# A decoder trunk on one Trainium2 core: four output chunks of w_out under way, and unread products in TensorE's longer planned gaps

## The chip, the core and the metric

The kernel runs as one program on one of the eight cores of a Trainium2 chip (trn2). The metric is the device time of one execution in microseconds. The engines are named as the profile names them: PE is TensorE (matrix products; PEld is its loading of weights), DVE is VectorE, ACT is ScalarE, POOL is GpSimd, SP is SyncE, whose queue issues the DMAs.

## The reference, cut to what matters

One inference step of a two-layer decoder for 256 prompt positions and 8 sample positions, that is 264 columns under the same weights. Layer 0 mixes tokens with a Mamba-2 SSD block, layer 1 with dilated attention; each layer then attends into 256 memory tokens and ends with a gated feed-forward block.

```python
for i in range(DEPTH):
    u = rms_norm(x, g[0])
    mix = ssd_mixer(u, ...) if i % 2 == 0 else dilated_mixer(u, ...)
    x = x + rms_norm(mix, g[1])
    kv = memory_kv(mem, ...)                   # rms_norm(mem) @ w_kv
    x = x + rms_norm(cross_attn(rms_norm(x, g[2]), kv, w_q, w_o), g[3])
    x = x + rms_norm(conv_ffn(rms_norm(x, g[4]), ...), g[5])
```

The change concerns the end of `ssd_mixer`, and the gaps of TensorE everywhere:

```python
gated = y * silu(z)                            # (264, 2048), four groups of 512
gated = gated * rsqrt(mean(gated * gated, per group) + EPS)
out = (gated * norm_w) @ w_out                 # 2048 -> 1024
```

## The kernel before, in words

Activations lie with channels on the partitions and the 264 positions in the free dimension, in chunks of 128 channels. Every weight block (128 x 1024 numbers, 512 KB) comes by DMA into `raw`; ACT casts it to `hi`, and DVE takes `lo = raw - hi`. Activations are split likewise (`uh`, `ul`; `gh`, `gl` for w_out). A product is three passes, hi by h, hi by l and lo by h, so one block of eight sub-blocks is 24 products of 128 x 264 into one accumulator in PSUM. `product` does that for each output chunk; `wsplit` loads and splits the weights.

PSUM has eight banks under four tags: `mm` 2, `s` 2, `t` 3, `f` 1. An output chunk holds a bank from its first product until it has been read out. A chunk normally goes under `mm`, so two are under way at once. The list `head` names other tags for the next chunks: its entry `('t', 'f')` means a bank of tag `t`, with weights from the buffers `rawf`, `hif` and `lof`, which the memory work shares.

w_out has eight output chunks with 16 sub-blocks each, four per group of gates. Group 3 is gated last: its sum of squares goes through PE (tile `s`), ACT and DVE make the reciprocal root (`r`, `r2`), DVE scales `xs`, and ACT and DVE split the result into `gh` and `gl`. The last quarter of every output chunk waits for that. `memkv(l)` works out the keys and values of the memory tokens: the sums of squares (`rawf` by `ones`), their root `memr`, the scaled and split memory (`ld`, `mh`, `ml`), and products into the one bank `f`. It is recorded "aside", so the planner may put it wherever PE has room. The first cross-attention reads its result back from DRAM (`o_memk`, `o_memv`).

The order of work isn't the order of the program. `program` records operations; `Plan.rank` and `Plan.latest` give each a priority from assumed costs, and `Plan.order` places them engine by engine, the most urgent ready one first. `Plan.run` does so several times and issues the order that its own costs call shortest. Buffers of one tag are handed out in the order in which they were recorded. The planner also assumes that PE is half as fast after little work: it adds up planned columns in slices of its time (`columns`, against the constants `WINDOW` and `COLUMNS`) and doubles the cost of a product accordingly. Each engine then works strictly in the issued order, and a waiting instruction holds up all behind it. Every operation is issued by one statement, line 626, so the profile's rows are told apart by tile names: `mm<-gh,hi` is a w_out product, `mm<-uhl,hi` one of the other projections.

Of the kernel before, what the change touches and what calls it, by code (L numbers as in the profile page):

```python
# [7 lines left out]
F32 = mybir.dt.float32  # L8
# [115 lines left out]
class Pool:  # L124
# [9 lines left out]
    def tile(self, shape, dt=F32, tag=None, bufs=1, name=None):  # L134
        b = Buf(self.plan, tuple(shape), dt, self, tag or name, bufs)
        b.name = name
        b.slots = self.last.setdefault(b.tag, Slots(bufs))
        return b.view

    def __enter__(self):  # L140
# [38 lines left out]
class Plan:  # L179
    def __init__(self, nc, tc):  # L180
        import concourse.bacc as bacc
        self.nc, self.tc = nc, tc
        self._nc2 = bacc.Bacc("TRN2", target_bir_lowering=False, num_devices=1)
        self.ops, self.stack, self.closed, self.loose, self.k = [], [], [], [None], 0
        self.follows, self.lengths, self.first = None, [], 0
        self.vector, self.scalar = Engine(self, "DVE", nc.vector), Engine(self, "ACT", nc.scalar)
        self.gpsimd, self.tensor = Engine(self, "POOL", nc.gpsimd), Engine(self, "PE", nc.tensor)
        self.sync, self.either = Engine(self, "SP", nc.sync), Either(self)
# [235 lines left out]
    def order(self, emit):  # L424
# [8 lines left out]
        columns = {}  # L433
# [46 lines left out]
        def open_pool(p):  # L480
# [13 lines left out]
                p.real = p.ctx.__enter__()  # L494
            real_stack.append(p)

        for o in self.ops:
            if o.n == 0:
                admit(o)
        left = len(self.ops)  # L500
        while left:
            best = None
            for e in engs:
                w, r = wait[e], ready[e]
                while w and w[0][0] <= free[e]:
                    _, _, o = heapq.heappop(w)
# [5 lines left out]
                if r:  # L512
                    s = free[e]
                elif w:
                    s = w[0][0]
# [6 lines left out]
            s, e = best  # L522
            w, r = wait[e], ready[e]
            free[e] = s
            while w and w[0][0] <= s:
                _, _, o = heapq.heappop(w)
                heapq.heappush(r, (o.prio, o.seq, o))
            o = None
            if e == "ACT":
# [15 lines left out]
                o = pick[2]  # L545
            elif e == "PE" and HOLD:

                k = int(s / WINDOW)
                rate = 2.4 if columns.get(k - 1, 0.0) >= COLUMNS else 1.2
                room = columns.get(k, 0.0) + (WINDOW * (k + 1) - s) * rate - COLUMNS  # L550
# [21 lines left out]
                o = pick[2]  # L572
            else:
                o = heapq.heappop(r)[2]
# [10 lines left out]
            late = max([max(min(b.slots.free)[0], b.pool.opens()) for b in o.bufs if b.real is None], default=0.0)  # L585
# [4 lines left out]
            for b in o.bufs:  # L590
                if b.real is None:
                    open_pool(b.pool)
                    place_ = min(b.slots.free)
# [11 lines left out]
            if e in ("DVE", "POOL") and o.port[e]:  # L605
                s = max(s, port)
                port = s + ns
            if e == "PE":
                if part not in (None, o.part):
                    ns += CHANGE  # L610
                part = o.part

                ns *= 1 if columns.get(int(s / WINDOW) - 1, 0.0) >= COLUMNS else 2
                k = int((s + ns) / WINDOW)
                columns[k] = columns.get(k, 0.0) + o.columns
            o.end, o.took = s + ns, ns
            free[e] = o.end
            if e == "SP":
                dma = max(dma, s + 1300.0) + o.nbytes / 320.0
                o.end = dma + 1000.0  # L620
                free[e] = max(free[e], dma - BACKLOG)
            if call is not None and emit:
                f, a, k = call
                a = [v.real() if isinstance(v, View) else v for v in a]
                k = {n: v.real() if isinstance(v, View) else v for n, v in k.items()}
# [26 lines left out]
WINDOW = 10240 / 3  # L652
COLUMNS = 3060.0
# [6 lines left out]
LATE_D = -1e6  # L660
# [9 lines left out]
CHANGE = 100.0  # L670
STRETCH = 2.5
HOLD = 12
PASSES = 4
SPARES = 2000.0, 3000.0, 5000.0
SWITCHES = 2000.0, 4000.0
# [24 lines left out]
def program(plan, A):  # L700
    V, S, G, PE, D, E = plan.vector, plan.scalar, plan.gpsimd, plan.tensor, plan.sync, plan.either
    with ExitStack() as ctx:
# [37 lines left out]
        x = ap_.tile([P, KD, T], F32, tag="x", name="x")  # L740
# [10 lines left out]
        D.dma_start(out=idf, in_=A["ident"])  # L751
        identr = cp.tile([P, P], F32R, name="identr")
        S.copy(identr, idf)
        ident = identr.bitcast(F32)

        idn2f = load(cp, "idn2")
# [23 lines left out]
        def product(w, kk, chunks, xh, xl, consume, late=None):  # L780

            for j in chunks:

                tag, own = head.pop(0) if head else ("mm", "")
                acc = pm.tile([P, 512], F32, tag=tag, name=nm("mm"), bufs=BANKS[tag])[:, :T]
                wv = w[j].rearrange("p (k c) -> p k c", k=kk)
                for k0 in range(0, kk, 8):
                    kn = min(8, kk - k0)
                    hi, lo = wsplit(wv[:, k0:k0 + kn, :], own, (2, 2) if own else (4, 3), late=late)
                    for k in range(kn):  # L790
                        PE.matmul(acc, hi[:, k, :], xh[:, k0 + k, :], start=k0 + k == 0, stop=False)
                        PE.matmul(acc, hi[:, k, :], xl[:, k0 + k, :], start=False, stop=False)
                        PE.matmul(acc, lo[:, k, :], xh[:, k0 + k, :], start=False, stop=k0 + k == kk - 1)
                consume(j, acc)
# [141 lines left out]
        def ssd(uh, ul, r):  # L936
            with plan.pool("ssd") as sp:
# [149 lines left out]
                t = small()  # L1087
# [157 lines left out]
                    pass  # L1245
                D.dma_start(out=A["o_pconv"], in_=pconv)
                D.dma_start(out=A["o_sconv"], in_=hist[:, :, 1:4, :])
                with plan.aside():
                    memkv(0)
                post = Post(1)  # L1250
                product(A["w_out"], 16, range(8), gh, gl, post, late=LATE_D)
                return post.finish(2)

        def states(pool):
# [663 lines left out]
```

## Time and profile before

| | |
|---|---|
| median of three runs | 1140.64 us (1138.1 to 1141.13) |
| the profiled execution | 1134.57 us |
| its span, first to last instruction | 1132.8 us |
| PE busy | 1032.3 us, 91% |
| DVE busy | 889.2 us, 78% |
| ACT busy | 642.2 us, 57% |
| mean granted clock of TensorE | 0.958 |

The profiled execution is 1.77 us longer than its span and 6.07 us shorter than the median of the other runs. In the rows below, busy time is what an engine worked in a stretch; the idle time in square brackets in a row of the timeline is what the engine waited just before it, with the instruction that ended the wait. PEclk is the granted clock as a share of full speed: 1.00 is 2.4 GHz and 0.50 is 1.2 GHz.

### The profile page before, as it was taken

What the parts mean: (1) busy time and instruction counts of PE and PEld (TensorE: products, weight loads), DVE (VectorE), ACT (ScalarE), POOL (GpSimd) and SP (SyncE); (2) the same over time, 40 slices, a digit from 0 to 9 for tenths busy, and PEclk for the clock granted to TensorE, in tenths of its full rate; (3) what the DMA queues carried; (4) which work ended last, traced back from release to release, by engine and by line L of the source; (5) the groups of instructions that cost most, each with busy time, mean ns of one, the idle gap of its engine ahead of it and who ended that gap; (6) DMA issues with size and microseconds to landing.
All of it is one profiled execution on the core that took longest, in us unless ns stands there. A gap on an engine that the chain in (4) does not pass through costs nothing.

```text
span 1132.8 us, 21191 instructions
## 1 busy us (share of the span) xinstructions
PE 1032.3 (91%) x7895; PEld 982.9 (87%) x7895; DVE 889.2 (78%) x2060; ACT 642.2 (57%) x1271; POOL 66.9 (6%) x142
## 2 busy tenths in 40 slices
PE   6799978979998698999999999999896989999995
PEld 6799866979988597999999999989795879999995
DVE  7989999974889889999954685574899778777544
ACT  7887665664644378777644554344544356555442
POOL 0221110000000000222200000000000001000000
PEclk9899988989999899999999999998998889999998
DMA  9234545665898876888767876676589336878761
GB/s 311 85 113 161 175 130 170 216 224 182 292 320 292 287 266 191 274 281 277 269 198 217 277 282 241 223 282 238 182 303 327 130 112 224 279 270 287 263 177 53
DMA packets 80599, 257.20 MB, mean 227 GB/s; under 512 B 16952, under 2 KB 21848, under 8 KB 79344
## 3 DMA queue, kind: packets, MB, share of 16 engines
q1 hardware_dynamic: 80496, 255.85, 66.6%
q8 instruction: 62, 1.02, 0.3%
q14 instruction: 41, 0.34, 0.1%
HBM read 238.70 MB, written 44.34 MB: 250 GB/s over the span
## 4 chain that ended last, share of the span: by engine, by line
PE 66%; DVE 18%; ACT 7%; DMA 6%; issue 3%; SPq 0%; DVEq 0%; ACTq 0%
PE mm L626 48%; PE s L626 7%; PE f L626 7%; DVE kv L626 4%; PE t L626 3%; DVE lo L626 3%; DMA o_sssm<-sto 2%; ACT hi L626 2%; DVE kvo L626 1%; DVE xs L626 1%; ACT L601 1%; ACT sto L626 1%; DVE yv L626 1%; DVE hif L626 1%; DMA raw<-w_in 1%
## 5 line engine op out<-in xcount | busy, mean ns | idle before, releaser
L626 PE MATMUL mm<-uhl,hi 128*128 128x264 f32 x2960 | 569.3, 290 | 33.5 <-ACT uhl L626 15.5
L626 PEld LDWEIGHTS mm<-uhl,hi 128*128 128x128 f32 x2960 | 468.6, 191 | 42.9 <-ACT uhl L626 17.3
L626 DVE TENSOR_TENSOR lo<-raw,hi 128x1024 fp32r<-128x1024 f32 (+1 forms) x283 | 338.4, 1197 | 136.5 <-ACT hi L626 131.4
L626 PE MATMUL mm<-uhl,lo 128*128 128x264 f32 x1480 | 423.1, 287 | 1.4 <-DVE lo L626 1.4
L626 ACT CAST hi<-raw 128x1024 fp32r<-128x1024 f32 (+1 forms) x283 | 291.6, 1033 | 226.7 <-PE mm L626 182.7
L626 PEld LDWEIGHTS mm<-uhl,lo 128*128 128x128 f32 x1480 | 281.3, 190 | 2.3 <-DVE lo L626 1.9
L626 PE MATMUL mm<-mh,lo 128*128 128x264 f32 x352 | 100.2, 285 | 0.0
L626 PE MATMUL mm<-mh,hi 128*128 128x264 f32 x352 | 100.0, 284 | 0.0
L626 PE MATMUL mm<-ml,hi 128*128 128x264 f32 x352 | 99.9, 284 | 0.0
L626 DVE SCALAR_TENSOR_TENSOR kv<-kv,t 128x256 f32<-128x256 f32 x256 | 88.9, 416 | 7.7 <-PE t L626 7.4
L626 PEld LDWEIGHTS mm<-mh,lo 128*128 128x128 f32 x352 | 66.4, 189 | 0.0
L626 PEld LDWEIGHTS mm<-ml,hi 128*128 128x128 f32 x352 | 66.2, 188 | 0.0
L626 PEld LDWEIGHTS mm<-mh,hi 128*128 128x128 f32 x352 | 66.2, 188 | 0.0
L626 PE MATMUL f<-mh,hi 128*128 128x256 f32 x128 | 39.0, 304 | 7.7 <-ACT hi L626 4.7
L626 ACT ACTIVATE sto<-t,sdt 128x128 f32<-128x128 f32 x128 | 37.9, 389 | 12.3 <-DMA o_sssm<-sto 11.0
L626 POOL COPY pst<-gr 128x2 f32<-128x2 f32 x44 | 27.0, 613 | 281.7 <-DVE gr L626 281.6
L626 PE MATMUL mm<-gh,hi 128*128 128x264 f32 x128 | 37.5, 296 | 6.3 <-ACT gh L626 6.3
L626 DVE SCALAR_TENSOR_TENSOR gy<-gr,ld,gy 128x255 f32<-128x255 f32 (+1 forms) x88 | 42.0, 480 | 1.0 <-ACT gy L626 0.8
L626 PE MATMUL f<-hi,ml 128*128 128x256 f32 x128 | 37.3, 291 | 3.2 <-ACT kvo L626 3.2
L626 PE MATMUL f<-hi,mh 128*128 128x256 f32 x128 | 37.3, 292 | 2.9 <-ACT kvo L626 2.9
L626 PE MATMUL f<-lo,mh 128*128 128x256 f32 x128 | 37.2, 290 | 2.7 <-DVE lo L626 1.6
L626 PE MATMUL f<-mh,lo 128*128 128x256 f32 x128 | 38.5, 301 | 0.5 <-DVE lo L626 0.5
(284 smaller groups left out, 1702.6 us busy)
## 6 DMA issues: line engine op xcount, KB each, us to landing
raw<-ffn_gu SPq DMA_DIRECT2D x88, 512.0 KB, 4.6
raw<-w_in SPq DMA_DIRECT2D x40, 512.0 KB, 3.7
kv<-cmk SPq DMA_DIRECT2D x32, 512.0 KB, 5.7
kv<-cmv SPq DMA_DIRECT2D x32, 512.0 KB, 5.9
raw<-ffn_d SPq DMA_DIRECT2D x32, 512.0 KB, 4.0
o_sc<-cache SPq DMA_DIRECT2D x16, 1022.0 KB, 8.3
raw<-w_qkv SPq DMA_DIRECT2D x18, 512.0 KB, 5.6
rawf<-state SPq DMA_DIRECT2D x16, 512.0 KB, 4.4
```

Of the source, the lines that this page charges most:

```text
L601: self.nc.scalar.preload_act_table_set(o.table)
L626: f(*a, **k)
```

## The change

Two things are changed. First, `ssd` records the product of w_out before the memory work of layer 0, and `head` gives its first four output chunks banks of their own: two under `mm`, two under `t`, the fourth with weights from the buffers of the memory work. Second, `order` calls a new function, `warm`, before it places an instruction on PE. Where PE's planned wait, shortened to 70 per cent, is at least 500 ns, and a bank of some tag is free at its start, it issues as many 512-column products of the identity matrix by itself as fit, at an assumed 215 or 430 ns each, and lets the planner count them. Nobody reads the result; the bank goes back afterwards. These tiles are named `keep`.

```diff
@@ class Pool, tile
         b.slots = self.last.setdefault(b.tag, Slots(bufs))
+        if self.psum:
+            self.plan.banks.setdefault(b.tag, b)
@@ class Plan, __init__
+        self.keep, self.banks, self.kept = None, {}, []
@@ class Plan, order
+        def warm(a, s):
+
+            s = a + FILL * (s - a)
+            tags = [(t, x.slots) for t, x in self.banks.items() if x.slots.free and min(x.slots.free)[0] <= a]
+            if s - a < GAP or not tags:
+                return a, ()
+            tag, slots = min(tags, key=lambda t: min(t[1].free)[0])
+            room, out = [], None
+            while True:
+                ns = (215.0 if columns.get(int(a / WINDOW) - 1, 0.0) >= COLUMNS else 430.0)
+                if a + ns > s:
+                    break
+                a += ns
+                room.append((int(a / WINDOW), 512.0))
+                if emit:
+                    if out is None:
+                        x = self.banks[tag]
+                        out = x.pool.real.tile([128, 512], F32, tag=tag, bufs=x.bufs, name="keep%d" % len(self.kept))
+                        self.kept.append(out)
+                    v = self.keep[0].real()
+                    self.nc.tensor.matmul(out, v, v.unsqueeze(1).to_broadcast([128, 4, 128]), start=True, stop=True)
+            if room:
+                place_ = min(slots.free)
+                slots.free.remove(place_)
+                slots.free.append((a + 380.0, place_[1], None))
+            return a, room
+
         for o in self.ops:
             if o.n == 0:
                 admit(o)
...
             if e == "PE":
+                if self.keep is not None and self.keep[1].end is not None:
+                    t, room = warm(max(last, self.keep[1].end + 300.0), s)
+                    if room:
+                        for k, n in room:
+                            columns[k] = columns.get(k, 0.0) + n
...
+FILL = 0.7
+GAP = 500.0
@@ program
         S.copy(identr, idf)
+        plan.keep = identr, plan.ops[-1]
@@ ssd
+                post = Post(1)
+                head[:] = [('mm', ''), ('mm', ''), ('t', ''), ('t', 'f')]
+                product(A["w_out"], 16, range(8), gh, gl, post, late=LATE_D)
                 with plan.aside():
                     memkv(0)
-                post = Post(1)
-                product(A["w_out"], 16, range(8), gh, gl, post, late=LATE_D)
```

The new order has 222 of these products in 46 groups, the longest of 17, 15, 14, 14, 14 and 10. Since the planner plans anew around them, other instructions move too. Three places follow. The first is PE at the end of gating. The tiles `mm_...<-gh` are output chunks of w_out; `s_451` is the sum of squares of group 3, `gh_454` is the scaled group 3 that comes of it, and `f_459<-rawf` are the sums of squares of the memory. Before:

```order
L626 MATMUL mm_558_2761<-gh_445_2780,lo_564_2789 128x264
L626 MATMUL f_459_2765<-rawf_465_2774,ones_60 128x256
L626 MATMUL s_451_2859<-sq_447_2803,ones_60 128x264
L626 MATMUL s_451_2859<-sq_450_2835,ones_60 128x264
L626 MATMUL f_459_2765<-rawf_467_2827,ones_60 128x256 x2
L626 MATMUL mm_550_2720<-gh_454_2889,hi_555_2678 128x264
```

And now, with two chunks more, `mm_473` and `mm_481`, the first three rows and the last five of the same stretch:

```order
L664 MATMUL s_451_2937<-sq_447_2895,ones_60 128x264
L664 MATMUL s_451_2937<-sq_450_2921,ones_60 128x264
L664 MATMUL mm_465_2849<-gh_445_2874,lo_471_2917 128x264
...
L664 MATMUL mm_481_2926<-gh_398_2528,lo_484_2941 128x264
L664 MATMUL mm_481_2926<-gh_398_2528,hi_483_2766 128x264
L664 MATMUL mm_481_2926<-gl_399_2533,hi_483_2766 128x264
L664 MATMUL mm_457_2805<-gh_454_3014,hi_462_2749 128x264
L664 MATMUL mm_465_2849<-gh_454_3014,hi_470_2852 128x264
```

Between the sum of group 3 and the first product that needs group 3 there were two rows of memory sums, and now there are 52 products of w_out; the memory sums stand some 200 products later. The second place is DVE at the same point: `r2` and `r` are the reciprocal root of group 3, `xs` the scaling by it, `memr` and `ld` belong to the memory, and `lo` is a weight split. Before:

```order
L626 TENSOR_TENSOR sq_447_2803<-sq_447_2803,sq_449_2816 128x264
L626 SCALAR_TENSOR_TENSOR r2_453_2875<-s_451_2859,r_452_2865 128x264
L626 SCALAR_TENSOR_TENSOR kvo_468_2877<-f_459_2765,memr_2871 128x256
L626 SCALAR_TENSOR_TENSOR r2_453_2875<-r2_453_2875,r_452_2865 128x264
L626 SCALAR_TENSOR_TENSOR kvo_468_2877<-kvo_468_2877,memr_2871 128x256
L626 SCALAR_TENSOR_TENSOR r_452_2865<-r2_453_2875,r_452_2865 128x264
L626 SCALAR_TENSOR_TENSOR memr_2871<-kvo_468_2877,memr_2871 128x256
L626 TENSOR_TENSOR xs_28_2087<-xs_28_2087,r_452_2865 128x1056
L626 SCALAR_TENSOR_TENSOR ld_469_2783<-ld_469_2783,ld_456_331,memr_2871 128x256 x2
L626 SCALAR_TENSOR_TENSOR ld_470_2838<-ld_470_2838,ld_456_331,memr_2871 128x256 x2
L626 SCALAR_TENSOR_TENSOR gl_455_2899<-xs_28_2087,ld_22_304,gh_454_2889 128x264 x4
```

Now:

```order
L664 TENSOR_TENSOR sq_447_2895<-sq_447_2895,sq_449_2906 128x264
L664 TENSOR_TENSOR lo_476_2934<-raw_474_2812,hi_475_2911 128x1024
L664 TENSOR_TENSOR lo_484_2941<-raw_482_2708,hi_483_2766 128x1024
L664 TENSOR_TENSOR lo_487_2957<-raw_485_2784,hi_486_2857 128x1024
L664 SCALAR_TENSOR_TENSOR r2_453_2980<-s_451_2937,r_452_2946 128x264
L664 SCALAR_TENSOR_TENSOR r2_453_2980<-r2_453_2980,r_452_2946 128x264
L664 SCALAR_TENSOR_TENSOR r_452_2946<-r2_453_2980,r_452_2946 128x264
L664 TENSOR_TENSOR xs_28_2132<-xs_28_2132,r_452_2946 128x1056
L664 TENSOR_TENSOR lo_479_3010<-raw_477_2841,hi_478_2991 128x1024
L664 SCALAR_TENSOR_TENSOR gl_455_3026<-xs_28_2132,ld_22_304,gh_454_3014 128x264 x4
```

The memory's seven operations have gone from between the sum and `gl`, and four weight splits for the new chunks have come, three of them ahead of the root. The third place is PE at the start of the last feed-forward block, where `s_1751` is the sum of squares after the cross-attention and the `mm` rows are the first products of the feed-forward block. Before:

```order
L626 MATMUL mm_1746_10935<-uhl_1692_10289,lo_1749_10880 128x264
L626 MATMUL s_1751_10970<-sq_1715_10745,ones_60 128x264
L626 MATMUL s_1751_10970<-sq_1750_10974,ones_60 128x264
L626 MATMUL mm_1770_10999<-uhl_1754_10993,hi_1772_10902 128x264
L626 MATMUL mm_1776_11002<-uhl_1754_10993,hi_1778_10937 128x264
```

Now:

```order
L664 MATMUL mm_1746_11181<-uhl_1692_10514,lo_1749_11126 128x264
L664 MATMUL s_1751_11216<-sq_1715_10987,ones_60 128x264
L520 MATMUL keep42_11225<-identr_136 128x512 x3
L664 MATMUL s_1751_11216<-sq_1750_11220,ones_60 128x264
L520 MATMUL keep43_11250<-identr_136 128x512 x14
L664 MATMUL mm_1770_11249<-uhl_1754_11243,hi_1772_11148 128x264
L664 MATMUL mm_1776_11267<-uhl_1754_11243,hi_1778_11183 128x264
```

Three and fourteen unread products have come into the chain, ahead of instructions that it waits for; the other rows stand as they did.

## Rows read from the trace of the kernel before

**Rows 1.** The page: busy time by engine, and the chain that ended last.
```profile
PE 1032.3 (91%) x7895; PEld 982.9 (87%) x7895; DVE 889.2 (78%) x2060; ACT 642.2 (57%) x1271; POOL 66.9 (6%) x142
PE 66%; DVE 18%; ACT 7%; DMA 6%; issue 3%; SPq 0%; DVEq 0%; ACTq 0%
```

**Rows 2.** Busy time by stage; columns: stretch, length, engines, PEclk, DMA share, GB/s.
```profile
60.00:120.00 60.00, 59.78 (x492) 56.82 (x492) 57.25 (x115) 46.63 (x93) 13.12 (x22) 1.00 0.47 156
120.00:213.00 93.00, 80.14 (x591) 70.09 (x591) 91.41 (x179) 52.03 (x100) 5.24 (x8) 0.91 0.50 157
213.00:228.00 15.00, 15.00 (x112) 14.56 (x112) 14.65 (x26) 13.96 (x21) 0.00 (x0) 1.00 0.69 231
284.00:360.00 76.00, 71.11 (x558) 68.57 (x558) 66.58 (x216) 40.03 (x80) 0.00 (x0) 1.00 0.89 306
924.00:960.00 36.00, 35.68 (x271) 35.29 (x272) 29.95 (x67) 22.00 (x42) 1.69 (x10) 0.94 0.45 160
```

**Rows 3.** Timeline of PE around the wait in w_out: start, us, instruction, [idle before].
```profile
228.15 1.05 PE L626 MATMUL s<-sq,ones 128*128 128x264 f32 x4
229.04 1.03 PE L626 MATMUL f<-rawf,ones 128*128 128x256 f32 x4
236.34 0.81 PE L626 MATMUL mm<-gh,hi 128*128 128x264 f32 x2 [6.28 <-ACT gh L626]
```

**Rows 4.** The chain that ended last, at full clock: start, us, what.
```profile
213.91 6.15 PE mm L626 x50
```

**Rows 5.** Timeline of DVE in the same wait, and one weight split from the chain.
```profile
230.92 0.43 DVE L626 SCALAR_TENSOR_TENSOR r<-s,r 128x264 f32<-128x264 f32 x1 [3.23 <-ACT r L626]
234.12 1.66 DVE L626 SCALAR_TENSOR_TENSOR ld<-ld,ld,memr 128x256 f32<-128x256 f32 x4
204.37 1.14 DVE lo L626
```

**Rows 6.** Stretches at half clock (columns as in rows 2); the sum is over all twelve.
```profile
37.67:44.50 6.83, 5.66 (x26) 5.69 (x27) 6.83 (x20) 5.89 (x14) 1.85 (x4) 0.50 0.00 1
160.55:170.79 10.24, 7.86 (x29) 6.21 (x30) 10.24 (x21) 3.25 (x8) 0.83 (x2) 0.50 0.63 133
191.27:198.10 6.83, 3.66 (x10) 1.99 (x11) 6.83 (x14) 3.06 (x7) 0.00 (x0) 0.50 0.03 11
232.23:242.47 10.24, 6.12 (x27) 6.10 (x28) 9.70 (x19) 7.22 (x14) 0.00 (x0) 0.50 0.35 122
382.42:392.66 10.24, 6.01 (x22) 5.27 (x23) 8.88 (x41) 2.00 (x5) 0.00 (x0) 0.50 0.92 354
430.21:433.62 3.41, 3.15 (x15) 2.84 (x14) 3.41 (x11) 3.06 (x9) 0.00 (x0) 0.50 0.89 292
873.94:887.59 13.65, 8.81 (x26) 6.72 (x27) 10.19 (x49) 4.89 (x15) 0.00 (x0) 0.50 0.75 264
921.73:928.55 6.82, 4.53 (x19) 4.49 (x20) 6.75 (x20) 3.25 (x9) 0.00 (x0) 0.50 0.17 64
sum 95.00, PE 62.86 PEld 55.00 DVE 75.14 ACT 36.59 POOL 2.68; mean PE 5.24 PEld 4.58 DVE 6.26 ACT 3.05 POOL 0.22
```

**Rows 7.** Timeline of PE: idle times, and 512-column products at full clock.
```profile
322.24 1.99 PE L626 MATMUL s<-ld,qT 128*128 128x256 f32 x8 [2.21 <-DMA ld<-o_memk]
422.91 1.05 PE L626 MATMUL t<-bB,sel 128*128 128x512 f32 x3
423.80 0.28 PE L626 MATMUL f<-mh,hi 128*128 128x256 f32 x1
429.25 0.50 PE L626 MATMUL t<-bB,sel 128*128 128x512 f32 x1 [3.41 <-ACT sto L626]
877.51 1.30 PE L626 MATMUL s<-identr,pp 128*128 128x128 f32 x4 [5.92 <-ACT pp L626]
924.02 1.47 PE L626 MATMUL mm<-uhl,hi 128*128 128x264 f32 x5 [4.13 <-ACT uhl L626]
```

**Rows 8.** The chain that ended last, in the cross-attention of layer 1.
```profile
882.74 7.73 PE s L626 x24
```

More of the change, by code (lines that the diff above doesn't have):

```diff
@@ L500, in order @@
         left = len(self.ops)
+        last = 0.0
         while left:
@@ L617, in order @@
             free[e] = o.end
+            if e == "PE":
+                last = o.end
             if e == "SP":
```

## The prediction

> **What bounds the kernel now.** I read the page first, then the busy time of the engines by stage, then the timeline of PE for its waits, and last the chain that ended last. On the page PE is busy for 1032.3 us of the span, 91%, and has two thirds of the chain [rows 1]. That average hides stages with other limits [rows 2]. From 120 to 213 us DVE works 91.41 us of 93 and PE 80.14: there DVE decides, and a quicker PE buys nothing. From 213 to 228 us, and from 924 to 960, PE is all but full and everything it doesn't have to do is worth its time. So a change to PE's waits and clock has to be priced stage by stage.
>
> The timeline of PE has few long waits. The longest are 6.28 us in w_out [rows 3], and 5.92 us and 4.13 us in and after the cross-attention of layer 1 [rows 7]. After such waits the granted clock falls: the half-clock stretches hold 95.00 us, in which PE is busy for 62.86 us [rows 6]. The last of them lies behind PE's last product and costs nothing.
>
> **w_out with four chunks.** In the trace PE sums the squares of group 3 at 228.15, finishes some memory sums, and then waits 6.28 us for `gh` [rows 3]. It had nothing left, because only two chunks were open and both had done their first three quarters. In the new order 52 products of two further chunks stand between that sum and the first product that needs group 3. Fifty such products took 6.15 us at full clock [rows 4], so 52 take 6.40 us, which fills the wait: 6.28 us go. With the wait goes the half clock behind it: from 232.23 to 242.47 PE is busy for 6.12 us [rows 6], which at 2.4 GHz in place of 1.2 would be 3.06 us. Together 9.3 us at the most.
>
> What comes late next is `gh` itself. Three weight splits now stand ahead of the root on DVE and one ahead of `gl`: 4 x 1.14 = 4.6 us [rows 5]. Seven memory operations have left: four took 1.66 us, and the three at 0.43 us like `r` are at most 1.3 us [rows 5]. That leaves DVE with some 1.6 us more, in a place where it sat idle for 3.23 us [rows 5]. If DVE is no earlier there than before, `gh` comes up to 1.6 us later than it did. On PE the memory's eight sums no longer lie ahead of that wait; of two passes each, at 1.03 us for four passes [rows 3], they are 4.1 us, which PE has done less of by then. So an idle rest of between 0 and 6.28 + 4.1 + 1.6 - 6.4 = 5.6 us can stay. I take 1.4 us, nearer to nothing: six of the eight stood ahead of group 3's sum, which is so issued 3.1 us earlier, and DVE's idle 3.23 us is more than its added work. Net gain 7.9 us, between 3.7 and 9.3. It is kept by what follows: w_out's end opens the next stage, and the loads of that stage wait for the buffers that w_out frees, so they move with it.
>
> **The unread products.** There are 222. I laid the groups beside the trace by the names of their neighbours: 22 groups with 136 products stand where PE waits, 24 groups with 86 where the trace shows no wait. Their length: three 512-column products start at 422.91 and the next product at 423.80, so 0.30 us each at the most [rows 7]. In a wait they cost nothing as long as they fit: 14 take at most 4.2 us, against 4.13 and 5.92.
>
> What they give is clock. A wait of 2.21 us stands in a stretch with PEclk 1.00 [rows 2, 7]; after 3.41 us the clock is at half from 430.21 [rows 6, 7]. Where the fill leaves less than that, I take the clock as kept.
>
> - After 924.02: the 14 fill the 4.13 us to the end, so 4.53 us of work at half clock [rows 6] becomes half as long: 2.3 us gained, on PE's path, since the products wait for nothing else there.
> - From 873.94 to 887.59: fourteen at 0.22 to 0.30 us leave 1.7 to 2.8 us of the 5.92, between the wait that kept the clock and the one that lost it. PE is busy 8.81 us in it and the chain runs over its 24 products of 7.73 us [rows 6, 8]. All of it would be 4.4 us; I take half, 2.2.
> - From 382.42 to 392.66: DVE is busy 8.88 of 10.24 us and PE 6.01 [rows 6]. At most 3.0 us; I take 0.9, since DVE sets the pace.
> - From 160.55 to 170.79 and from 191.27 to 198.10 DVE is busy to the last hundredth [rows 6]; from 37.67 to 44.50 also. Nothing, though the first product after the wait there could give up to 2.8 us.
>
> The 86 products outside a wait are work. Seventeen stand between 44 and 86 us and ten between 148 and 220. PE is full from 60 to 120, but its lateness falls to DVE, which is full after that and decides [rows 2]: nothing, with 17 x 0.30 = 5.1 us as the other end. Six of the ten stand at 214 to 221, where PE is full: 1.8 us in whole. Eleven stand at the start of the feed-forward block of layer 0 and in the memory work behind it, next to the wait of 3.41 us, and I take half, 1.6 us of 3.3. Seven stand at 941 to 945, where PE is busy 35.68 of 36 us [rows 2]: half again, 1.1 us of 2.1. The rest, in the two cross-attentions, wait beside DVE: nothing. Sum 4.5 us, between 0 and 12.3.
>
> **The sum.** -7.9 - 2.3 - 2.2 - 0.9 + 4.5 = -8.8 us. Against the profiled execution that is 1134.57 - 8.8 = 1125.8 us. That execution lay 6.07 us below the median of the other runs, so on the median I forecast 1140.64 - 8.8 = 1131.8 us. The terms' own ends give -21.8 us (9.3, 2.3, 4.4, 3.0 and 2.8 gained, nothing paid) and +8.6 us (3.7 gained, no clock, 12.3 paid), 1119 to 1149 us.
>
> **The rivals.**
>
> *The fills push the products (slower).* The planner lays fills into waits of its own making. Where the run has no such wait, a fill stands ahead of a real product on an engine that works in order, and each costs up to 0.30 us: 86 x 0.30 = 25.8 us. Against the gains of 13.3 us that is +12.5 us, 1153 us. It decides as soon as more than 44 of the 86 are paid in full. For it: PE's full stretches [rows 2]. Against it: 45 of the 86 lie beside work of DVE that sets the pace.
>
> *The gain of w_out is given back in the cross-attention of layer 0 (no change).* From 284 to 360 us the DMA engines are busy 0.89 of the time, and PE waits there 2.21 us for the read-back of the memory keys [rows 2, 7]. The memory sums now come some 200 products later, so their keys may come later too. If PE arrives 7.9 us sooner and waits as much longer there, the rest is -0.9 us, 1139.7 us. Against it: the first product of the keys stands where it stood, between the products of the last w_out chunk.
>
> *The fills don't hold the clock (the change doesn't do what it says).* Then the three clock terms go and the costs stay: -7.9 + 4.5 = -3.4 us, 1137.2 us. For it: the longest fills leave up to 2.8 us idle, which no row shows either way.
>
> *All the half clock counts.* If clock, not DVE, set the pace also where DVE is full, the seven stretches at a fill or at w_out would count whole: 6.83 + 10.24 + 6.83 + 10.24 + 10.24 + 13.65 + 6.82 = 64.85 us [rows 6], half of it 32.4 us. With 6.28 - 1.4 us of wait and the costs that is -32.8 us, 1107.8 us. Against it: in these stretches DVE is busy up to the full 10.24 of 10.24 us. The Trainium skill has this as a rule, in "TensorE: Matmul & The Clock Gate", section "Terms": the time at the lower clock, times the share of clock lost, is about the penalty. By that rule the sum is the one just given. The trace agrees where PE is full, as from 430.21 us (3.15 of 3.41 us), and doesn't show it where DVE is.
>
> **How the numbers follow.** A change under 0.3%, 3.4 us, can't be told from none with this kernel. Chances: the forecast 0.56; the given-back gain 0.16; the pushing fills 0.14; the clock not held 0.10; all the half clock 0.04. Faster gets nearly all of the forecast, 0.53, the last case, 0.04, and half of the case at -3.4 us, 0.05, with 0.04 of the given-back gain: 0.66. No change gets most of the given-back gain, half of the clock case, and a little of the forecast: 0.17. Slower gets the pushing fills and a little of the others: 0.17. The range runs from 1118 us, just past the forecast's best end, to 1147 us, near the terms' worst end and half way into the slower case.
>
> **What would show each step.** The wait ahead of `gh` at about 229 us should be under 1.5 us, and PEclk 1.00 from there to the end of w_out. Rows of `keep` should take some 0.22 us each at full clock. PEclk should stay at 1.00 at the start of the last feed-forward block. DVE should be as full as before from 120 to 213 us, and that stage not shorter by more than 2 us. The prediction is wrong if products behind a fill start later than their inputs allow, if the first cross-attention's wait for the memory keys grows by several us, or if w_out's wait only moves to the weight splits on DVE.

## The result, and the profile after

The changed kernel takes 1129.4 us in the median of eight executions; 1131.8 us were forecast. The kernel before has a median of 1137.41 us over eight, three of which are those of the section above. The five that ran beside the changed kernel have a mean of 1136.14 us, the changed kernel's eight one of 1129.03: a ratio of 0.9937, with an interval from 0.991 to 0.9964. On another occasion it gave 0.9935 (0.9907 to 0.9963). That is 7.2 us less, where 8.8 us were forecast. The profiled execution took 1124.51 us, 4.9 us under that median, with a mean granted clock of 0.988.

From the page after: busy time by engine, the chain that ended last, and the group of unread products, fills for short (busy us, mean ns of one, idle before).

```profile
PE 1066.2 (95%) x8117; PEld 1002.4 (89%) x8117; DVE 888.8 (79%) x2060; ACT 649.6 (58%) x1277; POOL 65.6 (6%) x142
...
PE 59%; DVE 25%; ACT 8%; issue 4%; DMA 4%; SPq 0%; DVEq 0%; ACTq 0%
...
L520 PE MATMUL keep<-identr 128*128 128x512 f32 x222 | 60.7, 403 | 0.0
```

Beside [rows 1], PE is busy for 34 us more in a shorter span, and yet its share of the chain fell from 66% to 59%, while DVE's rose from 18% to 25%. PE's own work became shorter, and more of the chain runs over DVE. The unread products overlap with their neighbours: 51.3 of the 60.7 us are time in which PE did nothing else, which leaves 1014.8 us for the products that are read, 17.5 less than before.

The same stretches as in [rows 2], after (columns as there).

```profile
60.00:120.00 60.00, 57.93 (x456) 53.23 (x455) 55.69 (x103) 49.78 (x97) 11.14 (x16) 1.00 0.47 154
120.00:213.00 93.00, 86.28 (x660) 75.56 (x658) 92.95 (x191) 54.52 (x103) 9.72 (x14) 1.00 0.53 165
213.00:228.00 15.00, 13.95 (x98) 12.64 (x99) 14.50 (x25) 11.90 (x17) 0.00 (x0) 1.00 0.71 219
284.00:360.00 76.00, 74.22 (x577) 70.85 (x577) 69.65 (x241) 41.25 (x84) 0.00 (x0) 1.00 0.90 312
924.00:960.00 36.00, 35.41 (x287) 34.78 (x286) 28.78 (x56) 22.24 (x35) 2.60 (x14) 1.00 0.66 234
```

PEclk is 1.00 in all of them. From 120 to 213 us DVE is still the engine that decides, at 92.95 of 93 us.

The timelines of PE and ACT where group 3 of the gates becomes ready, the place of [rows 3] (start, us, instruction, idle before): its sum of squares, its scaling into `gh`, and the first products that need it.

```profile
232.10 1.09 PE L664 MATMUL s<-sq,ones 128*128 128x264 f32 x4
...
237.93 1.74 ACT L664 ACTIVATE gh<-xs,ld 128x264 fp32r<-128x264 f32 x4 [0.23 <-DVE xs L664]
...
239.42 0.41 PE L664 MATMUL mm<-gh,hi 128*128 128x264 f32 x2
```

The 52 products of the two further chunks run from 232.83 to 239.42 us without a break, and the wait of 6.28 us for `gh` is gone. These are PE's waits in all of w_out (us in total, times, longest):

```profile
PE mm L664 <- DVE lo L664: 0.9, 2, 0.5
PE mm L664 <- ACT hi L664: 0.2, 1, 0.2
```

The two for weight splits on DVE lie at its start, at 221.76 and 226.19 us.

The stretches at half clock ahead of the program's tail, the answer to [rows 6]; these are all of them.

```profile
676.28:679.69 3.41, 3.41 (x18) 3.41 (x17) 1.12 (x6) 1.38 (x5) 0.00 (x0) 0.50 0.53 213
683.11:689.93 6.82, 6.82 (x34) 6.82 (x34) 0.72 (x3) 2.03 (x8) 0.00 (x0) 0.50 0.69 231
758.20:761.61 3.41, 3.41 (x16) 3.15 (x15) 1.90 (x6) 1.50 (x5) 0.00 (x0) 0.50 0.41 146
870.84:874.25 3.41, 3.41 (x11) 2.25 (x11) 3.41 (x23) 0.25 (x1) 0.00 (x0) 0.50 0.80 265
```

They are 17.1 us, where the kernel before has 85.3 ahead of its tail. In the second profile of the changed kernel they are 34.1 us: one profile gives one execution, and the mean clocks in the table of the experiments are the firmer numbers. The two long waits of [rows 7] in and after the cross-attention of layer 1, on the timeline of PE:

```profile
862.95 3.45 PE L520 MATMUL keep<-identr 128*128 128x512 f32 x14
869.52 0.33 PE L664 MATMUL s<-identr,pp 128*128 128x128 f32 x1 [3.12 <-ACT pp L664]
...
908.92 3.54 PE L520 MATMUL keep<-identr 128*128 128x512 f32 x14
913.41 0.75 PE L664 MATMUL mm<-uhl,hi 128*128 128x264 f32 x4 [0.95 <-ACT uhl L664]
```

Fourteen unread products take 3.45 us, 0.25 us each. The wait for `pp` is a little longer as a whole than the 5.92 us before (3.45 and 3.12 us): the fill pushed nothing there.

The stages, by the times at which they begin (us from the span's start). The changed kernel was profiled twice, and the two differ by 9.5 us.

| stage begins | before | after | after, again |
|---|---|---|---|
| first product of w_out | 216.65 | 221.02 | 221.38 |
| w_out ended | 280.27 | 276.61 | 277.03 |
| queries of layer 0 read out | 306.88 | 306.94 | 307.44 |
| cross-attention of layer 0 ended | 394.23 | 388.29 | 390.53 |
| feed-forward block of layer 0 | 448.13 | 444.02 | 446.43 |
| its down projection | 572.51 | 565.58 | 568.70 |
| qkv of layer 1 | 663.52 | 656.74 | 659.90 |
| queries of layer 1 read out | 814.98 | 807.76 | 815.40 |
| cross-attention of layer 1 ended | 896.90 | 886.30 | 894.97 |
| feed-forward block of layer 1 | 940.69 | 930.15 | 938.84 |
| end | 1132.79 | 1122.73 | 1132.18 |

w_out itself is 8 us shorter in both, 55.6 us in place of 63.6. But it begins 4.4 to 4.7 us later and the next stage is 3.7 us longer (with fills or without: it takes 30.3 to 30.4 us in e1 and e2 below too), so that at 307 us nothing is gained. The gain that lasts comes behind it.

### The profile page after: what moved, and what is told of

Same layout as the page of the kernel before. It is cut to its first block, busy times and chain, and to the rows that moved or that the text cites. A ratio compares the mean times of both kernels' runs of the same rounds, so it can differ in the third digit from the quotient of the medians.

```text
span 1122.7 us, 21633 instructions
## 1 busy us (share of the span) xinstructions
PE 1066.2 (95%) x8117; PEld 1002.4 (89%) x8117; DVE 888.8 (79%) x2060; ACT 649.6 (58%) x1277; POOL 65.6 (6%) x142
## 4 chain that ended last, share of the span: by engine, by line
PE 59%; DVE 25%; ACT 8%; issue 4%; DMA 4%; SPq 0%; DVEq 0%; ACTq 0%
PE mm L664 43%; PE f L664 7%; PE s L664 6%; DVE lo L664 5%; DVE kv L664 4%; PE t L664 3%; ACT hi L664 2%; DVE kvo L664 2%; DMA o_sssm<-sto 2%; DVE hif L664 2%; DVE xs L664 1%; DVE yv L664 1%; DVE r L664 1%; DMA raw<-w_in 1%; ACT L632 1%
## 5 line engine op out<-in xcount | busy, mean ns | idle before, releaser
L664 PE MATMUL mm<-uhl,hi 128*128 128x264 f32 x2960 | 561.9, 288 | 17.2 <-ACT uhl L664 11.5
L520 PE MATMUL keep<-identr 128*128 128x512 f32 x222 | 60.7, 403 | 0.0
L520 PEld LDWEIGHTS keep<-identr 128*128 128x128 f32 x222 | 39.2, 190 | 5.8
L664 PE MATMUL f<-mh,hi 128*128 128x256 f32 x128 | 36.7, 287 | 1.7 <-ACT kvo L664 1.7
```

Source lines behind the costliest of these rows:

```text
L520: self.nc.tensor.matmul(out, v, v.unsqueeze(1).to_broadcast([128, 4, 128]), start=True, stop=True)
L664: f(*a, **k)
```

## The experiments

All ratios are to the kernel before, on the same chip and at the same time. The clock is the mean of all executions of a kernel, the half clock that of its profiled one, ahead of the tail.

| kernel | ratio, 95% interval | unread products | mean clock | half clock, us |
|---|---|---|---|---|
| before | 1 | 0 | 0.957 | 85.3 |
| the change | 0.9937 (0.991 to 0.9964) | 222 | 0.985 | 17.1 |
| the change again (e9) | 0.9935 (0.9907 to 0.9963) | 222 | 0.985 | 34.1 |
| four chunks alone (e1) | 1.0042 (1.0017 to 1.0067) | 0 | 0.955 | 81.9 |
| the change's order, no fills (e2) | 1.0069 (1.0042 to 1.0096) | 0 | 0.956 | 85.3 |
| before, other table cost (e3) | 1.0177 (1.0143 to 1.0212) | 0 | 0.954 | 102.4 |
| fills behind w_out only (e4) | 0.9988 (0.9959 to 1.0016) | 175 | 0.976 | 34.1 |
| before's order, fills (e5) | 0.9972 (0.9946 to 0.9999) | 182 | 0.980 | 34.1 |
| the same, 32 columns (e6) | 0.9989 (0.9965 to 1.0013) | 182 small | 0.957 | 85.3 |
| order of e1, fills (e7) | 0.9989 (0.9966 to 1.0013) | 150 | 0.975 | 51.2 |
| fills alone, planned (e8) | 1.0018 (0.9989 to 1.0048) | 255 | 0.984 | 27.3 |
| the change, other plan (e10) | 0.997 (0.994 to 0.9999) | 235 | 0.988 | 30.7 |
| as e10, whole wait filled (e11) | 0.9977 (0.9958 to 0.9996) | 379 | 0.988 | 17.1 |
| the change, 30 fills fewer (e12) | 0.9964 (0.9941 to 0.9986) | 192 | 0.984 | 27.3 |

**First question: what each part does by itself, and what the order alone does.** The first group of four ran with these expectations. The four chunks alone:

```diff
-GAP = 500.0
+GAP = 1e9
```

> The four chunks of w_out alone; no unread product is issued or planned (GAP so long that none fits). Theory A (table loads: the new plan's extra activation-table loads on ACT cost the gating stage its 4.4 us, the chunks gain about 8 us in w_out, the unread products some 6 us behind it): 15 loads ahead of the first scaled group against 13, so the first w_out product at 217 to 219 us, the wait for gh gone, the half clock behind it gone, all other half-clock stretches as before, ratio 0.992 to 0.996. Theory B (the unread products cost the gating stage its 4.4 us): first w_out product at 216 to 217 us, ratio 0.991 to 0.994. Theory C (the gain of w_out is given back in the cross-attention of layer 0): ratio 0.998 to 1.001.

The order of the change, with the fills planned but not issued:

```diff
-                if emit:
+                if False:
                     if out is None:
```

> The changed kernel's own order, planned with the unread products, of which none is issued. Theory A (table loads): the loads stay, 19 ahead of the first scaled group, so the first w_out product stays at 220 to 223 us; the half clock comes back behind the waits of PE, and the run is 4 to 10 us slower than the changed kernel, ratio to before 0.997 to 1.003. Theory B (the unread products cost the 4.4 us): the first w_out product comes back to 216 to 218 us; ratio 0.992 to 0.997.

The kernel before with the table cost that the planner chose for the change:

```diff
-SWITCHES = 2000.0, 4000.0
+SWITCHES = (2000.0,)
```

> The kernel before, whose planner may only use the threshold of 2000 ns for changing ACT's table (SWITCHES has that value alone), which is what the changed kernel's plan chose; 28 loads in place of 22, no unread product, w_out as before. Theory A (table loads): six loads more of 1.28 us, 7.7 us on ACT, of which some 4 to 5 us reach the end: first w_out product at 220 to 222 us, ratio 1.003 to 1.006. Theory B (the unread products): first w_out product at 216 to 217 us, ratio 0.999 to 1.001.

Fills only from the end of w_out's record on:

```diff
-        plan.keep = identr, plan.ops[-1]
...
                 product(A["w_out"], 16, range(8), gh, gl, post, late=LATE_D)
+                plan.keep = identr, plan.ops[-1]
```

> The changed kernel with unread products only behind the last product of w_out (32 groups, 175 products); its plan has 22 table loads, 13 ahead of the first scaled group, as before. Theory A: first w_out product at 216 to 218 us, w_out 8 us shorter, the later stages some 6 us shorter: ratio 0.985 to 0.990, better than the changed kernel's 0.9937. Theory B says the same. Theory C (what a new plan gives is chance, not the loads or the unread products): ratio 0.992 to 0.998, no better than the changed kernel.

Measured: 1.0042, 1.0069, 1.0177 and 0.9988. The main result is e2's. The order of the change without its fills, four chunks and all, is 7.8 us slower than the kernel before; the fills in that same order take off 15 us. So the change's gain comes from the fills, and what the new order does by itself costs half of it.

Theory B, that the fills cost the 4.4 us ahead of w_out, falls: without them the same order reaches the first product of w_out at 224.76 us, later still. Theory A fits that place alone (e2 is later still than its 220 to 223 us). The order of the change loads ACT's table 22 times ahead of that product, where the kernel before does so 16 times:

```profile
L632 ACT ACT_TABLE_LOAD x27 | 34.6, 1283 | 0.5
...
L664 ACT ACT_TABLE_LOAD x1 | 1.3, 1283 | 0.7 <-PEq L1949 0.7
```

That is 28 loads of 1.28 us in all; the kernel before has 22. With 16 loads in this stage (e4) w_out begins at 216.76 us, as before; with 18 (e1) at 219.15, with 20 (e8 and e10 below) at 219.46. No run moved the loads by themselves, so that they are the cause is argued, not shown. In e3 the kernel before, given the same table cost, loses 6.2 us in this stage and another 27 us from the down projection of layer 0 to the qkv of layer 1, where it has 145 products of memory work in place of 93: its ratio says more of the plan than of the loads.

For the totals of e1 and e4 theory A is wrong (it had both faster), and C is nearer: what w_out gains is given back, but not in the cross-attention alone. In e1 w_out ends 6.4 us earlier than before and the cross-attention too; then 5.8 us go ahead of the feed-forward block, with 50 products of memory work in place of 38 and 8.1 us of half clock in place of 3.4, and 2.8 us in it, where ten such products now stand that weren't there. (The profiled execution of e1, 1133.87 us, is the fastest of its twelve: it shows where w_out's gain goes, but not the 4.8 us of loss that the ratio has.) The block in e1:

```profile
447.61:574.78 127.17, 121.03 (x973) 119.56 (x973) 114.68 (x192) 88.88 (x184) 26.46 (x44) 0.99 0.78 262
```

The change's own plan has one of them there, and the stage is 5.6 us shorter than in e1, 4.9 in the second profile (the first profile of the change):

```profile
444.02:565.58 121.56, 121.05 (x983) 119.14 (x982) 114.87 (x194) 88.87 (x184) 27.18 (x44) 1.00 0.81 273
```

So each new plan moves the memory work, and a few microseconds go with it.

**Second question: what the unread products are worth, in an order that doesn't change.** The second group sets them into two other orders without letting the planner count them; only its last run lets it. In the order of the kernel before, with w_out's record as it was:

```diff
-                    if room:
-                        for k, n in room:
-                            columns[k] = columns.get(k, 0.0) + n
...
-            if room:
-                place_ = min(slots.free)
-                slots.free.remove(place_)
-                slots.free.append((a + 380.0, place_[1], None))
...
-                post = Post(1)
-                head[:] = [('mm', ''), ('mm', ''), ('t', ''), ('t', 'f')]
-                product(A["w_out"], 16, range(8), gh, gl, post, late=LATE_D)
                 with plan.aside():
                     memkv(0)
+                post = Post(1)
+                product(A["w_out"], 16, range(8), gh, gl, post, late=LATE_D)
```

> The kernel before with its own order on every engine, w_out with two chunks, and 182 unread products (512 columns each, in 32 groups) issued in its planned waits; nothing is planned anew. Theory 1, that the unread products are worth about 15 us by their clock, as the changed kernel stood to the same order without them (0.9937 to 1.0069): ratio to the kernel before 0.985 to 0.990, profiled span 1116 to 1121 us, and less than 30 us of half clock ahead of the tail where the kernel before has 85 us. Theory 2, that those 15 us belong to that other order (its waits were planned with the fills in them) and fills in an order that doesn't know them cost as much as they give: 0.997 to 1.002. Theory 3, the prediction's, that only half clock on PE's own path counts: -3 to -6 us, 0.995 to 0.997.

The same with small products:

```diff
-                    self.nc.tensor.matmul(out, v, v.unsqueeze(1).to_broadcast([128, 4, 128]), start=True, stop=True)
+                    self.nc.tensor.matmul(out[:, 0:32], v, v[:, 0:32], start=True, stop=True)
```

> As the run before, the same 182 unread products in the same places, but of 32 columns each in place of 512, so that they hardly work PE. If the gain is the clock that the work of the fills holds, the waits and the half clock stay as they were (about 85 us ahead of the tail), and the ratio is 0.998 to 1.002. If something else about an instruction in the wait helped (its semaphores, the queue that stays awake, the bank), the ratio equals that of the fills of 512 columns.

The first two deletions alone, so that w_out has four chunks:

> w_out with four chunks, in the order that the planner chooses without fills (the run with w_out alone, which took 1.0042 of the kernel before), and 150 unread products in 32 groups issued in its planned waits, with nothing planned anew. Theory 1 (fills worth about 15 us wherever they stand in waits): 0.989 to 0.993. Theory 2 (they help only where planned in): 1.002 to 1.006. Theory 3 (only PE's own path): 0.999 to 1.001.

And w_out's record as before, with the planner counting the fills:

> w_out with two chunks as before, but the planner counts the fills and plans anew around them: 255 unread products in 48 groups, 26 table loads of ACT where the kernel before has 22 and the changed kernel 28. Theory 1: the fills' 15 us less some 4 us that planning anew cost ahead of w_out: 0.989 to 0.994. Rival, that planning anew decides and gives some us either way: anything from 0.985 to 1.01, with the stages in which it loses holding other counts of memory products or of table loads than before. If w_out's four chunks are what made the changed kernel faster, it is 1.000 or above.

Measured: 0.9972, 0.9989, 0.9989 and 1.0018. Theory 1 falls: in the order of before the fills are worth 3.2 us (0.1 to 6.1), not 15; theory 3, the prediction's, comes nearest. e5's 0.9972 is a hair above its 0.997, just inside theory 2's span; e7's 0.9989 is a hair below its 0.999, and theory 2, which asked for 1.002 or more there, falls. Against e1, the same order without fills, e7 is 0.0053 or 6 us lower. That they work by the clock, e5 and e6 show at the wait of [rows 3]. With 512 columns:

```profile
228.97 3.79 PE L520 MATMUL keep<-identr 128*128 128x512 f32 x15
235.13 0.58 PE L657 MATMUL mm<-gh,hi 128*128 128x264 f32 x2 [2.37 <-ACT gh L657]
```

With 32:

```profile
229.82 1.93 PE L520 MATMUL keep<-identr 128*128 128x32 f32 x15
236.29 0.81 PE L657 MATMUL mm<-gh,hi 128*128 128x264 f32 x2 [4.54 <-ACT gh L657]
```

The second kernel keeps all 85.3 us of half clock, the first 34.1; the mean clocks over all executions are 0.957 and 0.980. But these 51.2 us less bring 1.9 us by the two ratios, which their intervals can't tell from nothing. The page's numbers show how little of it arrives: PE's read products take 1021.1 us in e5 and 1032.3 before, 11.2 less; what the span holds beside them, waits and unread products, went from 100.5 to 104.6 us. In the stage ahead of w_out 17 us less of half clock (6.8 for 23.9) made the stage 0.7 us shorter.

In e8 the fills alone, planned, made nothing faster, with 67 of them ahead of w_out, 20 table loads and 18 products of memory work in the first feed-forward block.

**Third question: is the order of the change a good one by chance?** The last group has the change again, two other plans with both parts, and the change without those fills that the next product followed at once.

> The changed kernel as it is, once more, on the chip and beside the runs on which the three others of this group stand. Expected under every theory: 0.991 to 0.9964, its first interval; outside of that, the first ratio was partly chance of the chip.

```diff
-SWITCHES = 2000.0, 4000.0
+SWITCHES = (4000.0,)
```

> The changed kernel with one assumed cost of the planner held at one of its two values (4000 for an ACT table switch, which the planner chose for the kernel before; for the changed kernel it chose 2000): another order with both parts of the change, 235 unread products in 43 groups, 26 table loads. Theory 1, that four chunks and planned fills together are worth their 0.6%: 0.990 to 0.996. Theory 2, that this order is a lucky one among several whose times lie half a per cent apart (the fills alone gave 1.0018, the four chunks alone 1.0042, fills behind w_out alone 0.9988): anywhere from 0.990 to 1.005, and then the time follows the waits and work of the stages and not the number of fills.

With that edit and this one:

```diff
-FILL = 0.7
+FILL = 1.0
```

> As the run with the other plan, but the whole planned wait filled in place of 70 per cent: 379 unread products in 58 groups. If fills pay by the clock alone, the half clock goes below 10 us ahead of the tail and the ratio is 0.002 under that of the other plan. If the fills that reach past their waits cost, it is 0.002 to 0.008 above it, since 144 more products of some 0.25 us are 36 us on an engine that works in order.

```diff
+DROP = 3, 4, 6, 13, 26, 27, 28, 31, 39, 40, 45
...
+                        if len(self.kept) not in DROP:
+                            out = x.pool.real.tile([128, 512], F32, tag=tag, bufs=x.bufs, name="keep%d" % len(self.kept))
```

> The changed kernel in its own order, without the 11 groups (30 of 222 unread products) behind which the next product started at once, so that they may have pushed it. By the trace of the same order without fills these groups reach 3.1 us past their waits. The prediction's term (fills outside a wait cost 4.5 us): 4 us less than the changed kernel beside it, a ratio lower by 0.003 to 0.004. If the pushed products have slack, or the clock that these fills hold is worth as much: no difference, within 0.002.

Measured: 0.9935, 0.997, 0.9977, 0.9964. The change's gain is its own and not the chip's. With the other plan it is half as large by the middle values, though the intervals overlap, and its first feed-forward block is again the long kind:

```profile
448.12:576.30 128.18, 124.72 (x1002) 121.66 (x1001) 114.42 (x192) 86.62 (x179) 28.61 (x44) 1.00 0.77 255
```

The memory products in it, by the groups of PE's instructions there:

```profile
L664 PE MATMUL f<-mh,lo 128*128 128x256 f32 x5 | 1.5, 301 | 0.8 <-DVE lo L664 0.8
L664 PE MATMUL f<-mh,hi 128*128 128x256 f32 x5 | 1.4, 279 | 0.0
L664 PE MATMUL f<-ml,hi 128*128 128x256 f32 x4 | 1.1, 279 | 0.0
```

In all kernels with 10 to 18 products of memory work there (e1, e4, e7, e8, e10, e11) the block takes 125.8 to 128.2 us up to its down projection; in those with one or two (the change, e2, e3, e9, e12) 120.2 to 123.0; the kernel before, e5 and e6, with none, take 124.4, 124.1 and 123.0. So the count alone doesn't give the time, since with none the block is no quicker than with one or two. Filling the whole wait (e11, again another order than e10's) added 144 unread products, and neither the mean clock (0.988 in both) nor the time (0.9977 to 0.997) moved. Dropping the 30 fills that seemed to push made nothing faster: 0.9964 beside 0.9935.

## Why the prediction was right, and where it was not

**The total.** -8.8 us forecast, -7.2 and -7.4 measured. That it is so near is luck. The sum has -7.9 us for w_out and -0.9 for the fills (-5.4 of clock, +4.5 of cost). Measured, the new order alone is +7.8 us (e2), and the fills in it are -15. These misses cancel.

**w_out, -7.9 us.** In its own stage this is right: 8.0 us shorter, the wait and the half clock behind it gone, and DVE's weight splits late next by 0.9 us in all. That it is right to a tenth is luck, since the stage also lost eleven products of memory work, some 1.4 us if 24 in a row take 3.08 us, as behind w_out in the changed kernel. The failed step is the sentence that the gain "is kept by what follows". With it goes a term that the sum put at nothing: the stage ahead of w_out, 4.4 to 4.7 us longer in the new order. Alone the four chunks make the kernel slower, 1.0042. The two reasons given (w_out's end opens the next stage, its buffers free the loads) are about that stage's inputs; what was missed is that memory work had stood in w_out's stage (24 products, now 13), and that the planner moves it all anew: 162 in place of 148 in the stage behind w_out, and in e1 ten in the feed-forward block, where PE had worked 119 of 124 us and the block became 2.8 us longer. That this work is the cause is argued; no run moved it alone. The rival of the given-back gain was near it, at other places than it named.

**The fills' clock, -5.4 us, and their cost, +4.5 us.** In the order of before the net is -3.2 us, where -5.4 without a cost was my sum. In the change's order it is -15 us (0.9937 to 1.0069), three times as much. Term by term:

- The start of the last feed-forward block, -2.3 us: wrong. The half clock is gone, but the stage from the end of the cross-attention to its first gate takes 43.8 us before and 43.9 us after, and 43.8 in e5. The trace of before had shown the PE products behind a wait for `uhl`, and I took them for the path. From there to the next sum of squares it takes as long at a clock of 0.75 (before, 56 products) as at 1.00 (after, 72), and DVE, which makes what is summed, is busy for all but 0.24 us of both:

```profile
924.02:933.17 9.15, 9.15 (x56) 9.10 (x57) 8.91 (x26) 5.72 (x15) 0.00 (x0) 0.75 0.01 2
913.41:922.63 9.22, 9.20 (x72) 8.99 (x73) 8.98 (x26) 5.80 (x15) 0.00 (x0) 1.00 0.01 2
```

  Against its own order without fills (e2, 45.1 us) the change has 1.2 us here.
- The cross-attention of layer 1, -2.2 us: 3.4 and 2.4 us in the two profiles, but with 69 memory products in place of 111. With the same 69 and no fills (e2) it takes 82.0 us, as long as before, so in that order the fills give 3.5 and 2.5; in e5 0.8.
- The cross-attention of layer 0, -0.9 us: 1.5 in e5. In the change it is 6.0 and 4.3 us, with 15 memory products fewer; but e2 has 5.2 of that without a fill.
- Nothing where DVE is full: 0.7 us in e5 in the stage ahead of w_out, right for that order. In the change's order it is 3.7 and 3.4 us against e2; DVE isn't full there without fills, as the rows under what stays open show.
- The 86 fills outside a wait, +4.5 us: wrong, and the error is one of method. I held the new fills against the waits of the old trace. The trace of the change's order without fills (e2) has a wait of 0.5 us or more at 37 of the 46 groups, 194 of the 222 fills. For example at the fill of fourteen shown above:

```profile
883.90 0.48 PE L664 MATMUL s<-identr,pp 128*128 128x128 f32 x1 [6.33 <-ACT pp L664]
```

  At 0.25 us each all fills together reach some 5.3 us past those waits, and e12 shows no cost of the ones that do.

**The rivals.** Pushing fills: refuted by e2 and e12. Fills that don't hold the clock: refuted by e5 against e6. All half clock counts: between kernels refuted. In the change's own order 15 us were measured with 68.2 us less of it (51.2 by the second profile), in the order of before 3.2 with 51.2 less. By the rule of the Trainium skill in "TensorE: Matmul & The Clock Gate", section "Terms", these would be 34.1 us (25.6) and 25.6 us as estimates; the measurement decides. The prediction's row from 430.21 us doesn't speak for the rule either, since DVE is busy there for 3.41 of 3.41 us.

**What stays open.** Why the same kind of fill is worth 15 us in one order and 3 in another. Part is shown: PE's read products became 22.2 us shorter from e2 to the change (15.1 by the second profile) and 11.2 us from before to e5, while waits and fills grew by 5.1 (7.5) and 4.2 us. The two kernels of each pair have the same instructions in the same order but for the fills, so their stages can be compared: from e2 to the change the stage ahead of w_out is 3.4 to 3.7 us shorter, the one from the cross-attention of layer 0 to the feed-forward block 2.4 to 2.6; from before to e5 these are 0.7 and 0.9. In the first one sees how. In e2 PE waits for `mem`, works on at half clock, and DVE, full in that place in the kernel before, now waits for PE (three rows of e2, then the same DVE instruction in the change):

```profile
199.01 2.04 PE L664 MATMUL s<-mem,bn 128*128 128x512 f32 x2 [3.32 <-DVE mem L664]
198.60:205.40 6.80, 6.14 (x24) 4.47 (x25) 5.72 (x12) 2.32 (x6) 0.00 (x0) 0.50 0.16 52
206.15 0.48 DVE L664 SCALAR_TENSOR_TENSOR xs<-xs,ld,s 128x256 f32<-128x256 f32 x1 [1.83 <-PE s L664]
...
202.40 0.48 DVE L664 SCALAR_TENSOR_TENSOR xs<-xs,ld,s 128x256 f32<-128x256 f32 x1
```

One may think that an order planned for full clock loses more without it; no run tells that apart from the chance of the order. And as the ratios of e8, e10 and e11 show, half of the gain may be this plan's luck with the memory work in the feed-forward block; that block's rows speak for it, but no run moved the memory work alone.

## What to carry to other kernels

Where a planner orders the work, a change is also a new plan, and here plans with the same parts (the change, e10, e11) lay up to 0.4 per cent apart: run the new order without the change's instructions, and the old order with them, before a gain is put down to either. A fill is to be held against the waits of the order in which it stands, not of the order before. In these runs returned clock was worth about its half where PE was full; elsewhere much of it came back as a wait for the other engines, and which engine is full in a place is a matter of the order too.

## What the hardware showed that was not expected

In the dilated attention of layer 1 the clock falls to half while PE has next to no wait. Two profiles of the same kernel differ there by that. The changed kernel, the stage and a stretch in it:

```profile
656.74:807.76 151.02, 148.77 (x1109) 135.60 (x1108) 98.66 (x251) 72.35 (x173) 0.00 (x0) 0.95 0.69 247
...
674.00:774.00 100.00, 99.99 (x742) 91.36 (x742) 56.68 (x159) 42.03 (x109) 0.00 (x0) 0.93 0.66 238
```

And again, the stage and its longest stretch at half clock:

```profile
659.90:815.40 155.50, 153.28 (x1108) 139.80 (x1107) 98.80 (x251) 72.19 (x173) 0.00 (x0) 0.92 0.67 237
...
760.33:773.98 13.65, 13.65 (x58) 12.61 (x59) 4.58 (x18) 2.34 (x7) 0.00 (x0) 0.50 0.29 82
```

PE works 99.99 of 100 us and is granted 0.93. The second profile has 23.9 us of half clock in the stage, the first 13.7, and the stage is 4.48 us longer: 0.44 us per us, close to the half. PE is busy for 148.77 of 151.02 us there, so little else can limit it. The two other kernels with this order fit between: e12 takes 152.25 us with 17.1 us of half clock, e2 154.92 with 20.5. The rule of the Trainium skill in "TensorE: Matmul & The Clock Gate", section "Terms", would give an estimate of 5.1 us for these 4.48 us, so between executions of one kernel it about agrees. There is hardly a wait left to fill. The same stage has 6.8 us of half clock in the profile of e5 and 13.7 in that of the kernel before, and 2.9 of the 7.0 us between those two profiles lie in it: so much of what e5's profile seems to gain may be the execution's and not the fills'. The time of an execution follows its clock in this way: the eight of the changed kernel run from 1122.09 us at a mean clock of 0.991 to 1134.32 us at 0.979. A profile therefore stands anywhere in some 12 us, and stage times of two profiles are to be compared with that in mind.
